# A low-rank update of 64 token tiles: 32x32 transposes of float16 pairs on VectorE and one block-diagonal projection for 16 tiles, in place of TensorE transposes

## The chip, the cores and the metric

The kernel runs on one core of one Trainium2 chip. The metric is the time of one execution on the device in microseconds; a profile's span runs from the first to the last instruction of the profiled execution.

## The reference

```python
batch, seq, d_model, r = 16, 512, 768, 16
def reference(x, A, B, scale):            # x (16, 512, 768), A (768, 16), B (16, 768), all float32; scale 0.5
    lora = np.matmul(np.matmul(x, A), B)
    return (x + scale * lora).astype(np.float32)
```

There are 8192 tokens, that is 64 tiles of 128 tokens with 768 numbers each. Read and written once, x and the output are 25.2 MB each.

## The kernel before

The 64 tiles are loaded in six parts of 2, 6, 8, 16, 16 and 16 tiles (`PARTS`). In a part of S tiles a partition holds S consecutive tokens, so that its row of a DMA is one piece of S x 3 KB. All six parts have room of their own in SBUF, and all loads and stores are issued from SyncE (SP), whose queue is worked off in program order: loads of parts 0 and 1, A and B, parts 2 to 4, then the last part, whose room first serves to prepare A and B (L87 to L93) and which is therefore loaded after that. A part is added to in place and stored from the same tile; the two last parts are stored in halves of 8 tiles (`STORES`).

The work goes by chunks of four tiles (`CHUNK`). For a chunk and each of the six blocks of 128 columns, TensorE transposes the four 128x128 float32 pieces into PSUM against an identity (`transposed`, L113), and ScalarE copies them to SBUF as float16 (L115). `projected` (L122) sums six matmuls with A as the weights into a 16x512 tile, and VectorE scales it to float16 (L127). `added` multiplies this with B (L139, a 512 and a 256 column matmul for each tile) and VectorE adds the 128x768 result to x in place (L145). The main loop puts the transposes of chunk c around the additions of chunk c-1, so that TensorE has work while ScalarE and VectorE empty PSUM. GpSimd only clears the room for A and makes the identity. `finished` issues the store of a part, or half, behind its last addition (L155).

Of the kernel before, what the change touches and what calls it, by code (L numbers as in the profile page):

```python
# [1 line left out]

# [6 lines left out]


MM_DT = mybir.dt.float16

PARTS = [2, 6, 8, 16, 16, 16]

STORES = {4: [8, 8], 5: [8, 8]}

CHUNK = 4


@with_exitstack  # L20
def kernel(
    ctx: ExitStack,
    tc: tile.TileContext,
    x: bass.AP,
    A: bass.AP,
    B: bass.AP,
    scale: bass.AP,
    out: bass.AP,
):

    nc = tc.nc
    fp32 = mybir.dt.float32
    P = 128

    x2 = x.flatten_outer_dims()
    out2 = out.flatten_outer_dims()
    T, D = x2.shape
    R = A.shape[1]  # L40
    ND = D // P
    assert D % P == 0 and sum(PARTS) * P == T
    n_splits = [(n0, min(512, D - n0)) for n0 in range(0, D, 512)]
    sc = float(scale)

    const = ctx.enter_context(tc.tile_pool(name="const", bufs=1))
    xpool = ctx.enter_context(tc.tile_pool(name="xp", bufs=1))
    xtpool = ctx.enter_context(tc.tile_pool(name="xtp", bufs=6))
    ypool = ctx.enter_context(tc.tile_pool(name="yp", bufs=2))
    ps_xt = ctx.enter_context(tc.tile_pool(name="ps_xt", bufs=3, space=bass.MemoryType.PSUM))  # L50
    ps_y = ctx.enter_context(tc.tile_pool(name="ps_y", bufs=1, space=bass.MemoryType.PSUM))
    ps_l = ctx.enter_context(tc.tile_pool(name="ps_l", bufs=2, space=bass.MemoryType.PSUM))


    parts = []
    tok = 0
    for i, S in enumerate(PARTS):
        parts.append([None, tok, S])
        tok += S * P

    def rows(t2, i):
        _, tok0, S = parts[i]
        return t2[ds(tok0, S * P), :].rearrange("(p s) d -> p s d", s=S)

    def loaded(i):
        S = parts[i][2]
        parts[i][0] = xpool.tile([P, S, D], fp32, name=f"x_sb{i}")
        nc.sync.dma_start(out=parts[i][0], in_=rows(x2, i))  # L68


    last = len(parts) - 1
    lastpool = ctx.enter_context(tc.tile_pool(name="lastp", bufs=1))
    room = lastpool.tile([P, parts[last][2], D], fp32, name="room", tag="last")
    NB = D // 32
    a_rows = room[0:32, 0, 0 : 32 * R].rearrange("b (a r) -> b a r", r=R)
    a_t = room[0:32, 1, 0 : 32 * R].rearrange("a (r b) -> a r b", r=R)
    b_f32 = room[0:R, 2, :]
    nc.gpsimd.memset(a_rows, 0.0)  # L78
    loaded(0)
    loaded(1)  # L80
    nc.sync.dma_start(out=a_rows[0:NB, :, :], in_=A.rearrange("(b a) r -> b a r", a=32))
    nc.sync.dma_start(out=b_f32, in_=B)
    for i in range(2, last):
        loaded(i)


    nc.vector.transpose(out=a_t, in_=a_rows.rearrange("b a r -> b r a"))  # L87
    a_mm = const.tile([P, ND, R], MM_DT, name="a_mm")
    a_tv = a_t[:, :, 0:NB].rearrange("a r (c k) -> a k c r", k=4)
    for k in range(4):  # L90
        nc.vector.tensor_copy(out=a_mm[ds(32 * k, 32), :, :], in_=a_tv[:, k, :, :])  # L91
    b_mm = const.tile([R, D], MM_DT, name="b_mm")
    nc.vector.tensor_copy(out=b_mm, in_=b_f32)  # L93

    parts[last][0] = lastpool.tile([P, parts[last][2], D], fp32, name="x_last", tag="last")
    nc.sync.dma_start(out=parts[last][0], in_=rows(x2, last))

    ident = const.tile([P, P], fp32, name="ident")
    make_identity(nc, ident)


    chunks = [
        (i, s0, min(CHUNK, S - s0))
        for i, (_, _, S) in enumerate(parts)
        for s0 in range(0, S, CHUNK)
    ]
    state = {}

    def transposed(c, j):
        i, s0, n = chunks[c]  # L110
        xt_ps = ps_xt.tile([P, CHUNK, P], fp32, name="xt_ps")
        for s in range(n):
            nc.tensor.transpose(xt_ps[:, s, :], parts[i][0][:, s0 + s, ds(j * P, P)], ident)  # L113
        xt_sb = xtpool.tile([P, CHUNK * P], MM_DT, name="xt_sb")
        nc.scalar.copy(out=xt_sb[:, 0 : n * P], in_=xt_ps[:, 0:n, :])  # L115
        state[c, j] = xt_sb

    def projected(c):
        n = chunks[c][2] * P
        ps_yt = ps_y.tile([R, CHUNK * P], fp32, name="ps_yt")  # L120
        for j in range(ND):
            nc.tensor.matmul(  # L122
                ps_yt[:, 0:n], a_mm[:, j, :], state.pop((c, j))[:, 0:n],
                start=(j == 0), stop=(j == ND - 1),
            )
        yt_sb = ypool.tile([R, CHUNK * P], MM_DT, name="yt_sb")
        nc.vector.tensor_scalar(  # L127
            out=yt_sb[:, 0:n], in0=ps_yt[:, 0:n], scalar1=sc, scalar2=None,
            op0=mybir.AluOpType.mult,
        )  # L130
        state[c] = yt_sb

    def added(c, subs):
        i, s0, n = chunks[c]
        subs = [s for s in subs if s < n]
        lora = {s: ps_l.tile([P, D], fp32, name="lora_ps") for s in subs}
        for s in subs:
            for n0, w in n_splits:
                nc.tensor.matmul(  # L139
                    lora[s][:, ds(n0, w)], state[c][:, ds(s * P, P)], b_mm[:, ds(n0, w)],  # L140
                    start=True, stop=True,
                )
        for s in subs:
            xs = parts[i][0][:, s0 + s, :]
            nc.vector.tensor_tensor(out=xs, in0=xs, in1=lora[s], op=mybir.AluOpType.add)  # L145

    def finished(c):
        i, s0, n = chunks[c]
        del state[c]
        end = 0  # L150
        for w in STORES.get(i, [parts[i][2]]):
            end += w
            if end == s0 + n:
                piece = slice(end - w, end)
                nc.sync.dma_start(out=rows(out2, i)[:, piece, :], in_=parts[i][0][:, piece, :])  # L155

    for c in range(len(chunks)):
        for j in range(3):
            transposed(c, j)
        if c >= 1:  # L160
            added(c - 1, (0, 1))
        for j in range(3, ND):
            transposed(c, j)
        if c >= 1:
            added(c - 1, (2, 3))
            finished(c - 1)
        projected(c)
    c = len(chunks) - 1
    added(c, (0, 1))
    added(c, (2, 3))  # L170
    finished(c)


# [1 line left out]
_INS = ['x', 'A', 'B', 'scale']  # L175
_OUTS = [((16, 512, 768), 'float32')]

_NUMBERS = {'scale': 0.5}


# [26 lines left out]
```

## Time and profile before

| | |
|---|---|
| time, median of 3 runs | 125.39 us (125.31 to 129.49) |
| span of the profiled execution | 123.3 us (its own time stands nowhere else; it is one such execution) |
| TensorE busy, matmul | 99.2 us (80%), 614 instructions |
| TensorE weight loads | 62.0 us (50%) |
| VectorE busy | 70.4 us (57%), 87 instructions |
| ScalarE busy | 52.7 us (43%), 103 instructions |
| GpSimd busy | 1.2 us (1%) |
| DMA | 50.54 MB, mean 410 GB/s over the span; the SP queue's packets took 96.5% of 16 engines' span |
| mean granted TensorE clock | 0.920 |

Busy shares are averages over the whole span. In a group's line the two numbers after the count are the busy time in us and the mean of one instruction in ns; behind the second bar stands the idle time of the engine just before these instructions, and what ended it.

### The profile page before, as it was taken

The page shows a single profiled execution, that of the slowest core. Times are in us where ns is not written, and L with a number is a line of the kernel's source. Part 1 is how long each engine was busy: PE and PEld are TensorE (multiplying, and loading weights), DVE is VectorE, ACT ScalarE, POOL GpSimd, SP SyncE. Part 2 cuts the span into 40 slices and gives each one's busy share as a digit, 9 for nine tenths or more (in the row PEclk, how much of TensorE's full clock was granted, in tenths as well). Part 3 has the DMA queues.
Part 4 walks back from the last instruction along what each step waited for, and adds up shares of the span by engine and source line. Part 5 has one row for each costly group of instructions (what it writes and reads, how often), then busy time and mean ns, then how long its engine had stood idle before and what let it go on. Part 6 is the DMA issues. An engine that isn't in the chain of part 4 may idle for free.

```text
span 123.3 us, 1614 instructions
## 1 busy us (share of the span) xinstructions
PE 99.2 (80%) x614; PEld 62.0 (50%) x614; DVE 70.4 (57%) x87; ACT 52.7 (43%) x103; POOL 1.2 (1%) x7
## 2 busy tenths in 40 slices
PE   0363999999949999999999999999999999851000
PEld 0343655566518674747475656665665747320000
DVE  0004465954886048686867577686868686884000
ACT  4060464375505555546373737364555555400000
POOL 3000000000000000000000000000000000000000
PEclk9998599999997699999999999999999999995555
DMA  4999999899989969989899999989989999998991
GB/s 155 446 407 411 399 510 478 351 436 510 415 351 510 478 290 510 452 367 446 255 421 452 432 425 526 415 383 510 388 367 438 430 423 430 425 460 359 470 399 64
DMA packets 2092, 50.54 MB, mean 410 GB/s; under 512 B 252, under 2 KB 252, under 8 KB 548
## 3 DMA queue, kind: packets, MB, share of 16 engines
q1 hardware_dynamic: 2084, 50.43, 96.5%
q8 instruction: 5, 0.08, 0.3%
q14 instruction: 3, 0.02, 0.0%
HBM read 25.26 MB, written 25.17 MB: 409 GB/s over the span
## 4 chain that ended last, share of the span: by engine, by line
PE 73%; DMA 8%; DVE 8%; issue 1%; ACT 0%; SPq 0%; ACTq 0%
PE xt_ps L113 39%; PE lora_ps L139 18%; PE ps_yt L122 17%; DMA x_sb<-in_x_dram 8%; DVE x_last L145 4%; DVE x_sb L145 3%; DVE yt_sb L127 1%; ACT xt_sb L115 0%; SPq L68 0%; ACTq L115 0%
## 5 line engine op out<-in xcount | busy, mean ns | idle before, releaser
L115 ACT CAST xt_sb<-xt_ps 128x512 f16<-128x512 f32 (+1 forms) x102 | 51.5, 567 | 52.6 <-PE xt_ps L113 46.5
L145 DVE TENSOR_TENSOR x_sb<-x_sb,lora_ps 128x768 f32<-128x768 f32 x48 | 43.5, 951 | 17.3 <-PE lora_ps L139 17.3
L113 PE MATMUL xt_ps<-ident,x_sb 128*128 128x128 f32 x288 | 40.9, 296 | 8.5 <-DMA x_sb<-in_x_dram 8.4
L113 PEld LDWEIGHTS xt_ps<-ident,x_sb 128*128 128x128 f32 x288 | 34.3, 150 | 17.5 <-issue 12.6
L139 PE MATMUL lora_ps<-b_mm,yt_sb 16*128 16x512 f16 (+1 forms) x128 | 27.0, 326 | 3.8 <-DVE yt_sb L127 1.6
L122 PE MATMUL ps_yt<-xt_sb,a_mm 128*16 128x512 f16 (+1 forms) x102 | 24.4, 376 | 0.0
L145 DVE TENSOR_TENSOR x_last<-x_last,lora_ps 128x768 f32<-128x768 f32 x16 | 14.5, 951 | 5.4 <-PE lora_ps L139 5.3
L139 PEld LDWEIGHTS <-yt_sb 16*128 16x128 f16 x128 | 9.5, 92 | 15.0 <-issue 7.5
L127 DVE TENSOR_SCALAR yt_sb<-ps_yt 16x512 f16<-16x512 f32 (+1 forms) x17 | 10.9, 642 | 8.5 <-PE ps_yt L122 8.5
L122 PEld LDWEIGHTS <-a_mm 128*16 128x16 f16 x102 | 7.9, 91 | 13.3 <-issue 5.2
L113 PE MATMUL xt_ps<-ident,x_last 128*128 128x128 f32 x96 | 12.2, 277 | 0.0
L113 PEld LDWEIGHTS xt_ps<-ident,x_last 128*128 128x128 f32 x96 | 10.3, 140 | 3.0 <-PE ps_yt L122 1.7
L87 DVE STREAM_TRANSPOSE room<-room 32x512 f32<-32x512 f32 x1 | 1.0, 1037 | 10.8 <-DMA room<-in_A_dram 10.8
L115 ACT ACT_TABLE_LOAD x1 | 1.3, 1283 | 0.7 <-PEq L188 0.7
L91 DVE CAST a_mm<-room 32x96 f16<-32x96 f32 x4 | 0.9, 233 | 0.1
L93 DVE CAST b_mm<-room 16x768 f16<-16x768 f32 x1 | 0.5, 549 | 0.0
L78 POOL MEMSET room<- 32x512 f32 x1 | 0.5, 515 | 0.3 <-POOLq L188 0.3
masks.py:199 POOL TENSOR_SCALAR_AFFINE_SELECT ident<-ident 128x128 f32<-128x128 f32 x1 | 0.3, 294 | 0.1
masks.py:197 POOL MEMSET ident<- 128x128 f32 x1 | 0.2, 194 | 0.0
L188 POOL MEMSET const-bfloat16-1.0<- 128x1 bf16 x1 | 0.1, 102 | 0.0
L188 POOL MEMSET const-uint8-127<- 128x1 uint8 x1 | 0.1, 102 | 0.0
L188 POOL MEMSET const-float32-0.0<- 128x1 f32 x1 | 0.1, 99 | 0.2 <-issue 0.2
(1 smaller groups left out, 0.1 us busy)
## 6 DMA issues: line engine op xcount, KB each, us to landing
x_sb<-in_x_dram SPq DMA_DIRECT2D x2, 6144.0 KB, 38.0
out_dram<-x_sb SPq DMA_DIRECT2D x3, 3072.0 KB, 19.9
x_last<-in_x_dram SPq DMA_DIRECT2D x1, 6144.0 KB, 50.9
out_dram<-x_sb SPq DMA_DIRECT2D x1, 6144.0 KB, 26.5
out_dram<-x_last SPq DMA_DIRECT2D x2, 3072.0 KB, 11.7
x_sb<-in_x_dram SPq DMA_DIRECT2D x1, 3072.0 KB, 15.9
x_sb<-in_x_dram SPq DMA_DIRECT2D x1, 2304.0 KB, 9.9
out_dram<-x_sb SPq DMA_DIRECT2D x1, 2304.0 KB, 44.7
```

Of the source, the lines that this page charges most:

```text
L78: nc.gpsimd.memset(a_rows, 0.0)
L87: nc.vector.transpose(out=a_t, in_=a_rows.rearrange("b a r -> b r a"))
L91: nc.vector.tensor_copy(out=a_mm[ds(32 * k, 32), :, :], in_=a_tv[:, k, :, :])
L93: nc.vector.tensor_copy(out=b_mm, in_=b_f32)
L113: nc.tensor.transpose(xt_ps[:, s, :], parts[i][0][:, s0 + s, ds(j * P, P)], ident)
L115: nc.scalar.copy(out=xt_sb[:, 0 : n * P], in_=xt_ps[:, 0:n, :])
L122: nc.tensor.matmul(ps_yt[:, 0:n], a_mm[:, j, :], state.pop((c, j))[:, 0:n], start=(j == 0), stop=(j == ND - 1),)
L127: nc.vector.tensor_scalar(out=yt_sb[:, 0:n], in0=ps_yt[:, 0:n], scalar1=sc, scalar2=None, op0=mybir.AluOpType.mult,)
L139: nc.tensor.matmul(lora[s][:, ds(n0, w)], state[c][:, ds(s * P, P)], b_mm[:, ds(n0, w)], start=True, stop=True,)
L145: nc.vector.tensor_tensor(out=xs, in0=xs, in1=lora[s], op=mybir.AluOpType.add)
L188: nc = _bacc.Bacc("TRN2", target_bir_lowering=False, num_devices=1)
```

## The change

TensorE no longer transposes. x is first narrowed to float16 in SBUF (`narrowed`, four tiles at once, 128x3072; even blocks on ScalarE, odd ones on GpSimd, L114). Two float16 neighbours are then read as one 32-bit word, and VectorE transposes the 32x32 blocks of these words in place (`turned`, 128x1536 words, L118). After that, partition 32b+i holds, for every block c of 64 columns, columns 64c+2i and 64c+2i+1 of the 32 tokens of band b. A block-diagonal matrix with A four times on its diagonal (`w_bd`, 24 matrices of 128x128, one for each c and each half k of the pair) projects all four bands at once: 24 matmuls (`projected`, L129) sum one PSUM tile of 128 x 32n for a whole group of n tiles, their moving operand being every second float16. `spread` (L140, four ScalarE instructions on 32 partitions each) scales it to float16 into the diagonal blocks of `y_bd`, and `raised` (L150) multiplies 128x128 pieces of that with B, which stands four times in `b_mm`. One VectorE addition (L157) takes two tiles, 128x1536.

The groups have 4, 12, 16, 16 and 16 tiles. There is one `xh` for all groups, two `y_bd`, two PSUM tiles for the projections and two of three banks for `raised`.

The parts are now 8, 8, 16, 16, 8 and 8 tiles, the first loaded in two halves. Parts 4 and 5 use the room of parts 0 and 1: they are loaded, from SP, after the stores of these have landed (L162 and L73), and each part is stored whole. A and B are loaded from ScalarE's queue; GpSimd clears `w_bd`, `b_mm` and both `y_bd`.

The built program holds VectorE's work in this order, T being a `turned` of four tiles and A an addition of two (the bars part the groups whose additions they are; the first T belongs to group 0, and the T's between additions of one group are turns of the next): T AA | TTT AAAAATTTTA | AATTATATAAAA | AAAATTAAATTA | AAAAAAAA. It differs for groups 1 and 3 from the order in which the source lists them. On TensorE all raised pairs of groups 1 and 3 stand ahead of the next projection; in group 2 the projection is cut in three pieces of 8 matmuls around the last two pairs.

```diff
...
 import concourse.tile as tile
 from concourse import bass_utils, mybir
 from concourse.bass import ds, ts
-from concourse.masks import make_identity
 from concourse._compat import with_exitstack
 MM_DT = mybir.dt.float16
-PARTS = [2, 6, 8, 16, 16, 16]
-STORES = {4: [8, 8], 5: [8, 8]}
-CHUNK = 4
+PARTS = [8, 8, 16, 16, 8, 8]
+ROOM = ["a", "b", "c", "d", "a", "b"]
+LOADS = {0: [4, 4]}
+GROUPS = [4, 12, 16, 16, 16]
+SUB = 4
 @with_exitstack
...
     scale: bass.AP,
     out: bass.AP,
 ):
     nc = tc.nc
     fp32 = mybir.dt.float32
     P = 128
+    Q = 32
     x2 = x.flatten_outer_dims()
     out2 = out.flatten_outer_dims()
     T, D = x2.shape
     R = A.shape[1]
-    ND = D // P
-    assert D % P == 0 and sum(PARTS) * P == T
-    n_splits = [(n0, min(512, D - n0)) for n0 in range(0, D, 512)]
+    NC = D // 64
+    GMAX = max(GROUPS)
+    assert sum(PARTS) * P == T and sum(GROUPS) == sum(PARTS)
     sc = float(scale)
     const = ctx.enter_context(tc.tile_pool(name="const", bufs=1))
     xpool = ctx.enter_context(tc.tile_pool(name="xp", bufs=1))
-    xtpool = ctx.enter_context(tc.tile_pool(name="xtp", bufs=6))
-    ypool = ctx.enter_context(tc.tile_pool(name="yp", bufs=2))
-    ps_xt = ctx.enter_context(tc.tile_pool(name="ps_xt", bufs=3, space=bass.MemoryType.PSUM))
-    ps_y = ctx.enter_context(tc.tile_pool(name="ps_y", bufs=1, space=bass.MemoryType.PSUM))
+    ypool = ctx.enter_context(tc.tile_pool(name="yp", bufs=1))
+    ps_y = ctx.enter_context(tc.tile_pool(name="ps_y", bufs=2, space=bass.MemoryType.PSUM))
     ps_l = ctx.enter_context(tc.tile_pool(name="ps_l", bufs=2, space=bass.MemoryType.PSUM))
     parts = []
+    where = []
     tok = 0
     for i, S in enumerate(PARTS):
         parts.append([None, tok, S])
+        where += [(i, s) for s in range(S)]
         tok += S * P
     def rows(t2, i):
...
     def loaded(i):
         S = parts[i][2]
-        parts[i][0] = xpool.tile([P, S, D], fp32, name=f"x_sb{i}")
-        nc.sync.dma_start(out=parts[i][0], in_=rows(x2, i))
...
+        t = xpool.tile([P, S, D], fp32, name=f"x_sb{i}", tag=ROOM[i])
+        parts[i][0] = t
+        end = 0
+        for w in LOADS.get(i, [S]):
+            nc.sync.dma_start(out=t[:, ds(end, w), :], in_=rows(x2, i)[:, ds(end, w), :])
+            end += w
+    a_rows = const.tile([Q, 64 * R], fp32, name="a_rows")
+    a_t = const.tile([Q, 2, R, Q], fp32, name="a_t")
+    b_f32 = const.tile([R, D], fp32, name="b_f32")
+    w_bd = const.tile([P, NC, 2, P], MM_DT, name="w_bd")
+    b_mm = const.tile([P, D], MM_DT, name="b_mm")
+    xh = const.tile([P, GMAX, D], MM_DT, name="xh")
+    y_bd = [const.tile([P, GMAX, P], MM_DT, name=f"y_bd{i}") for i in range(2)]
+    nc.vector.memset(a_rows, 0.0)
     loaded(0)
-    loaded(1)
-    nc.sync.dma_start(out=a_rows[0:NB, :, :], in_=A.rearrange("(b a) r -> b a r", a=32))
-    nc.sync.dma_start(out=b_f32, in_=B)
-    for i in range(2, last):
+    nc.scalar.dma_start(out=b_f32, in_=B)
+    nc.scalar.dma_start(out=a_rows[0:NC, :], in_=A.rearrange("(c e) r -> c (e r)", e=64))
+    for i in range(1, 4):
         loaded(i)
-    nc.vector.transpose(out=a_t, in_=a_rows.rearrange("b a r -> b r a"))
-    a_mm = const.tile([P, ND, R], MM_DT, name="a_mm")
...
+    nc.gpsimd.memset(w_bd.rearrange("p c k m -> p (c k m)").bitcast(fp32), 0.0)
+    nc.gpsimd.memset(b_mm.bitcast(fp32), 0.0)
+    for t in y_bd:
+        nc.gpsimd.memset(t.rearrange("p s m -> p (s m)").bitcast(fp32), 0.0)
+    nc.vector.transpose(
+        out=a_t.rearrange("i k r c -> i (k r) c"),
+        in_=a_rows.rearrange("c (i k r) -> c (k r) i", k=2, r=R),
+    )
+    for b in range(P // Q):
+        nc.vector.tensor_copy(
+            out=w_bd[ds(b * Q, Q), :, :, ds(b * Q, R)],
+            in_=a_t[:, :, :, 0:NC].rearrange("i k r c -> i c k r"),
+        )
+    for b in range(P // Q):
+        nc.vector.tensor_copy(out=b_mm[ds(b * Q, R), :], in_=b_f32)
+    starts = [sum(GROUPS[:g]) for g in range(len(GROUPS))]
+    def narrowed(g, q):
+        i, s = where[starts[g] + q * SUB]
+        engine = nc.gpsimd.tensor_copy if q % 2 else nc.scalar.copy
+        engine(out=xh[:, ds(q * SUB, SUB), :], in_=parts[i][0][:, ds(s, SUB), :])
+    def turned(q):
+        v = xh[:, ds(q * SUB, SUB), :].bitcast(fp32)
+        nc.vector.transpose(out=v, in_=v)
     state = {}
-    def transposed(c, j):
-        i, s0, n = chunks[c]
...
+    def projected(g, steps):
+        n = GROUPS[g]
+        if g not in state:
+            state[g] = ps_y.tile([P, GMAX * Q], fp32, name="ps_yt")
+        xv = xh.rearrange("p s (c j k) -> p s c j k", c=NC, k=2)
+        for m in steps:
+            c, k = divmod(m, 2)
             nc.tensor.matmul(
-                ps_yt[:, 0:n], a_mm[:, j, :], state.pop((c, j))[:, 0:n],
-                start=(j == 0), stop=(j == ND - 1),
+                state[g][:, 0 : n * Q].rearrange("p (s j) -> p s j", j=Q),
+                w_bd[:, c, k, :], xv[:, 0:n, c, :, k],
+                start=(m == 0), stop=(m == 2 * NC - 1),
             )
-        yt_sb = ypool.tile([R, CHUNK * P], MM_DT, name="yt_sb")
-        nc.vector.tensor_scalar(
...
+    def spread(g):
+        n = GROUPS[g]
+        y = state.pop(g).rearrange("p (s j) -> p s j", j=Q)
+        for b in range(P // Q):
+            q = ds(b * Q, Q)
+            nc.scalar.mul(out=y_bd[g % 2][q, 0:n, q], in_=y[q, 0:n, :], mul=sc)
+    lora = {}
+    def raised(g, p):
+        t = ps_l.tile([P, 2, D], fp32, name="lora_ps")
+        lora[g, p] = t
+        for h in range(2):
+            lhsT = y_bd[g % 2][:, 2 * p + h, :]
+            for n0, w in ((0, 512), (512, 256)) if h == 0 else ((0, 256), (256, 512)):
                 nc.tensor.matmul(
-                    lora[s][:, ds(n0, w)], state[c][:, ds(s * P, P)], b_mm[:, ds(n0, w)],
-                    start=True, stop=True,
+                    t[:, h, ds(n0, w)], lhsT, b_mm[:, ds(n0, w)], start=True, stop=True
                 )
-        for s in subs:
-            xs = parts[i][0][:, s0 + s, :]
...
+    def added(g, p):
+        i, s = where[starts[g] + 2 * p]
+        xs = parts[i][0][:, ds(s, 2), :]
+        nc.vector.tensor_tensor(out=xs, in0=xs, in1=lora.pop((g, p)), op=mybir.AluOpType.add)
+    def finished(g, p):
+        i, s = where[starts[g] + 2 * p]
+        if s + 2 == PARTS[i]:
+            nc.sync.dma_start(out=rows(out2, i), in_=parts[i][0])
+            if i == 1:
+                loaded(4)
+                loaded(5)
+    MMS = 2 * NC
+    last = len(GROUPS) - 1
+    for q in range(GROUPS[0] // SUB):
+        narrowed(0, q)
+        turned(q)
+    projected(0, range(MMS))
+    spread(0)
+    raised(0, 0)
+    for g in range(len(GROUPS)):
+        pairs = GROUPS[g] // 2
+        subs = GROUPS[g + 1] // SUB if g < last else 0
+        for q in range(subs):
+            narrowed(g + 1, q)
+        order = ["a", "a"]
+        p_left, q_left = pairs - 2, subs
+        while q_left or p_left:
+            if q_left:
+                order.append("t")
+                q_left -= 1
+                if q_left == subs - 1 and q_left and p_left:
+                    order.append("t")
+                    q_left -= 1
+            if p_left:
+                order.append("a")
+                p_left -= 1
+        p = q = 0
+        done = 0
+        after = 0
+        rest = sum(1 for o in order[max(i for i, o in enumerate(order) if o == "t"):] if o == "a") if subs else 0
+        for o in order:
+            if o == "t":
+                turned(q)
+                q += 1
+                continue
+            if p + 1 < pairs:
+                raised(g, p + 1)
+            if q == subs and subs:
+                after += 1
+                to = min(MMS, -(-MMS * after // max(1, rest - 1)))
+                projected(g + 1, range(done, to))
+                done = to
+            added(g, p)
+            finished(g, p)
+            p += 1
+        if subs:
+            projected(g + 1, range(done, MMS))
+            spread(g + 1)
+            raised(g + 1, 0)
 # ---- launch: one core; inputs and outputs as the reference has them ----
```

More of the change, by code (lines that the diff above doesn't have):

```diff
@@ L66, in loaded @@
         S = parts[i][2]
-        parts[i][0] = xpool.tile([P, S, D], fp32, name=f"x_sb{i}")
-        nc.sync.dma_start(out=parts[i][0], in_=rows(x2, i))
[L71 to L77, printed above, removed]
@@ L78 @@
-    nc.gpsimd.memset(a_rows, 0.0)
+        t = xpool.tile([P, S, D], fp32, name=f"x_sb{i}", tag=ROOM[i])
[8 more added lines that the diff above has]
+    w_bd = const.tile([P, NC, 2, P], MM_DT, name="w_bd")
@@ L84 @@
+    for i in range(1, 4):
         loaded(i)
-    nc.vector.transpose(out=a_t, in_=a_rows.rearrange("b a r -> b r a"))
-    a_mm = const.tile([P, ND, R], MM_DT, name="a_mm")
[L89 to L106, printed above, removed]
-    state = {}
-    def transposed(c, j):
-        i, s0, n = chunks[c]
[L111 to L121, printed above, removed]
+    nc.gpsimd.memset(w_bd.rearrange("p c k m -> p (c k m)").bitcast(fp32), 0.0)
[6 more added lines that the diff above has]
+    )
@@ L124, in projected @@
-                start=(j == 0), stop=(j == ND - 1),
-            )
-        yt_sb = ypool.tile([R, CHUNK * P], MM_DT, name="yt_sb")
[L127 to L136, printed above, removed]
-        for s in subs:
-            for n0, w in n_splits:
+                state[g][:, 0 : n * Q].rearrange("p (s j) -> p s j", j=Q),
@@ L139, in added @@
                 nc.tensor.matmul(
-                    lora[s][:, ds(n0, w)], state[c][:, ds(s * P, P)], b_mm[:, ds(n0, w)],
-                    start=True, stop=True,
-                )
-        for s in subs:
-            xs = parts[i][0][:, s0 + s, :]
[L145 to L171, printed above, removed]
+                    t[:, h, ds(n0, w)], lhsT, b_mm[:, ds(n0, w)], start=True, stop=True
+                )
```

## The prediction

> **What bounds the kernel now.** I read the page's forty slices first, for which resource is full; then the end of the timeline, for what sets the last microseconds; then the groups by form, for prices; then the chain and the clock by microsecond, for how a burst of TensorE runs after a pause. The slices (tenths busy; the DMA row is the mean of 16 engines):
>
> ```profile
> PE   0363999999949999999999999999999999851000
> DVE  0004465954886048686867577686868686884000
> DMA  4999999899989969989899999989989999998991
> ```
>
> Two resources are full. DMA moves 50.5 MB at a mean of 410 GB/s over the span; TensorE is busy from slice 5 on. VectorE has room: 70.4 us of 123.3. The end of the timeline (start, duration):
>
> ```profile
> 108.79 3.66 DVE L145 TENSOR_TENSOR x_last<-x_last,lora_ps 128x768 f32<-128x768 f32 x4 [0.59 <-PE lora_ps L139]
> ...
> 112.48 0.33 SPq L155 DMA_DIRECT2D out_dram<-x_last  x1
> ```
>
> The last add ends at 112.45 and the span 10.85 us later, with the store of 8 tiles. The changed kernel also ends with a store of 8 tiles, so I forecast when its last add ends and put 10.9 behind it. The prices (busy us, mean ns of one):
>
> ```profile
> L115 ACT CAST xt_sb<-xt_ps 128x512 f16<-128x512 f32 x90 | 47.3, 593 | 46.5 <-PE xt_ps L113 40.7 <-PE ps_yt L122 5.7
> L145 DVE TENSOR_TENSOR x_sb<-x_sb,lora_ps 128x768 f32<-128x768 f32 x48 | 43.5, 951 | 17.3 <-PE lora_ps L139 17.3
> ...
> L127 DVE TENSOR_SCALAR yt_sb<-ps_yt 16x512 f16<-16x512 f32 x15 | 10.1, 673 | 6.8 <-PE ps_yt L122 6.8
> ...
> L115 ACT CAST xt_sb<-xt_ps 128x256 f16<-128x256 f32 x12 | 4.2, 375 | 6.1 <-PE xt_ps L113 5.8
> ...
> L87 DVE STREAM_TRANSPOSE room<-room 32x512 f32<-32x512 f32 x1 | 1.0, 1037 | 10.8 <-DMA room<-in_A_dram 10.8
> L91 DVE CAST a_mm<-room 32x96 f16<-32x96 f32 x4 | 0.9, 233 | 0.1
> L127 DVE TENSOR_SCALAR yt_sb<-ps_yt 16x256 f16<-16x256 f32 x2 | 0.8, 408 | 1.7 <-PE ps_yt L122 1.7
> L93 DVE CAST b_mm<-room 16x768 f16<-16x768 f32 x1 | 0.5, 549 | 0.0
> L78 POOL MEMSET room<- 32x512 f32 x1 | 0.5, 515 | 0.3 <-POOLq L188 0.3
> masks.py:199 POOL TENSOR_SCALAR_AFFINE_SELECT ident<-ident 128x128 f32<-128x128 f32 x1 | 0.3, 294 | 0.1
> masks.py:197 POOL MEMSET ident<- 128x128 f32 x1 | 0.2, 194 | 0.0
> ```
>
> TensorE's prices come from the chain (start, us, what), where the same work stands once after a pause and once in full flow; the second fence is the clock by microsecond (PE, PEld, DVE, ACT and POOL busy, then the granted clock):
>
> ```profile
> 11.20 2.54 PE xt_ps L113 x12
> 13.74 1.33 PE ps_yt L122 x6
> ...
> 23.19 1.46 PE xt_ps L113 x12
> ...
> 26.86 1.39 PE ps_yt L122 x6
> ...
> 29.72 0.75 PE lora_ps L139 x4
> ```
> ```profile
> 12.00:13.00 1.00, 1.00 (x7) 1.00 (x6) 0.93 (x5) 0.00 (x0) 0.00 (x0) 0.50 1.09 467
> ...
> 15.00:16.00 1.00, 1.00 (x8) 0.70 (x8) 0.41 (x1) 0.96 (x3) 0.00 (x0) 1.00 0.92 393
> ```
>
> After an idle of 3.2 us the clock fell to 0.50 and was whole again 3.8 us after work resumed. Six 256-column matmuls took 1.33 then, six of 512 columns take 1.39 later: 0.232 us per 512 columns warm, 0.443 cold.
>
> **The change, part by part.** *Removed:* 384 TensorE transposes (53 us busy), their 102 ScalarE copies, 17 VectorE scalings. TensorE's bound is gone: warm, it has four times 24 projections of 0.232 (22 us) and 32 raised pairs of 0.75 (24 us). Bytes are unchanged, so the DMA bound stays about where the span is now; not much can be won.
>
> *VectorE* becomes the serial engine, with 32 adds of 1536 elements and 16 turns of 1536. The two scalings differ by 265 ns for 256 elements, 1.035 ns each; an add of 768 is then 156 + 795, and one of 1536 is 1.75 us. A turn is bounded above by the only transpose here: (1037-156)/512 = 1.72 ns per element, 2.80 us. But that one reads 64 bytes apart. The strided CAST pays (233-156)/96 = 0.80 ns where the dense one pays (549-156)/768 = 0.51, a factor 1.6, and 1.72 is 1.66 times 1.035. So I take the dense turn at 1.035, that is 1.75 us. Below that would be the cast's 0.51 (0.94 us), which L87 speaks against: strided against strided it is twice the cast. The Trainium skill (SBUF — State Buffer, section on Door 1) says that SBUF reads at full rate while accesses share a 16-byte line and pays at each new line: by it the dense turn costs 1.75 (sum 146), by L87's own rate 2.80 (sum 163); that line is why L87 would be dear, and no run yet shows a dense turn.
>
> *ScalarE* narrows nine blocks of 3072: slope (593-375)/256 = 0.852, fixed 157, so 2.77 us each. Its four spreads per group (32x512) are 593 each, 2.37 together. *GpSimd* narrows seven blocks: between the memset's slope (515-194)/384 = 0.836 ns (2.66 us) and the select's (294-87)/128 = 1.62 (5.05 us); I take 5.05, the row that also reads. Neither binds: in a group that starts at T the first ScalarE block is ready at T+5.1 and wanted at T+6.6; the second GpSimd block at T+10.1, wanted at T+15. Cover is lost above some 7.5 us a GpSimd block; then the third and fourth turn are late by the excess.
>
> *The hand-over.* Projection g+1 needs all turns of g+1, because each matmul runs over every tile of the group; then four spreads, then one raised pair, then VectorE may add. What VectorE still has to add after its last turn is the only cover, and the built program decides it. Its VectorE order (T turn, A add) is: T AA | TTT | AAAAATTTTA | AATTATATAAAA | AAAATTAAATTA | AAAAAAAA. Behind the last T stand 0, 0, 1, 4 and 1 adds. TensorE has paused meanwhile (its raised pairs wait for adds), so I start projections cold.
>
> *The start.* A and B move to ScalarE's queue; before, A landed at 10.8 behind 3 MB. Alone it could land near the first load's 4.4 us: B at 4.5, A at 5.5 (bounds 4.5 and 10.8). Then four casts to b_mm at 0.55, the transpose of 32x1024 strided at 1.72 (1.92), four scatters of 768 at 0.80 (0.77 each): weights at 11.7 to 12, taken as 11.9 (up to 2.6 more if a scatter runs at 1.72, up to 4.3 if A is late).
>
> *The sum*, in us from the span's start.
> - Turn to 13.65; 24 cold projections of 128 columns, weight loads showing, 3.3 (bounds 2 and 4.5); four spreads of 0.27; a cold raise 1.5: first add at 19.5, AA to 23.0.
> - TTT to 28.25 (x1 lands by 18.5, as the same 6 MB do now). Projection of 384 columns, 3.8 cold, 6.05: 34.3; spreads 1.94; raise: 37.0.
> - AAAAATTTT to 52.75; x1 finished at 54.5. Projection 3.8 cold + 15.4 x 0.232 = 7.4: 60.15; spreads 62.5; raise 63.3.
> - AATTATAT to 77.3. Under the four adds TensorE does 8 projections cold (3.54), a pair, 8, a pair, 8: 86.1; x2 finished at 86.0; spreads and raise: 89.25.
> - Eleven more to 108.5, x3 finished at 110.25; projection 7.4, spreads 2.37, raise 0.75: 119.0.
> - Eight adds: 133.0. With 10.9: span 143.9, and 2.1 that the median stands above this span now (125.4 against 123.3): 146.0.
>
> Of the 133.0, 84 is VectorE's adds and turns, 12 the start, 37 waits at five hand-overs (6, 9, 9, 3, 9, rounded).
>
> *DMA against this.* 18.9 MB at 410 GB/s after 18.5 for the first third: x3 in at 49.3. The store of x0 is issued at 40.5 and lands near 57, that of x1 near 64; on SP the load of x4 waits for the first and that of x5 for the second, landing near 71 and 79, wanted at 89 and later. Behind those two loads on SP stands x2's store, wanted only at 86. DMA then idles from 79 to 86, and before x3's store: the loss is idle DMA, not more bytes.
>
> **The rivals.**
> - *Projections at twice the price* (0.14): the clock never rises in thin bursts, or the moving operand, every second fp16, streams at the fp32 transposes' 0.95 ns a column (1.46/1536). Cold throughout adds 2.0, 3.2, 4.8, 3.2: 159; at 0.95 up to 163. For it: TensorE is busy a third of the time. Against: 3.8 us of work sufficed above.
> - *Turns at L87's rate* (0.14): 16 x 1.05 more, 163. For: the only transpose row. Against: its stride.
> - *Warm and early* (0.04): all projections warm take off 8.7, an early A two more: 135 to 137.
> - *The other side: the hand-over is short* (0.06). Place: L129 and L140 between last turn and first add. If all 37 us went, DMA would bind again near 123 to 126. It decides from 20.6 us off the 37, about 5 of the 9 at each long one. Against: spreads and raise alone are 3.1 by rows, 24 warm projections 5.6. No row gives it.
> - *The late loads bite* (0.02): x4 and x5 land 10 us or more after my 71 and 79, so that the last group's turns wait; 150 to 156. Against: 18 us of slack.
>
> **How the numbers follow.** The forecast, 146 (its own range 138 to 154), has 0.60. The range for 8 in 10 reaches down to the warm case, 136, and up through both dear cases, 164. Some 2% is what a measurement of this kernel can tell from no change, so faster is below 122.9 and slower above 127.9. Only the short hand-over gets under 127.9; of its 0.06 I give 0.04 to the DMA bound at 123 to 127.9 (same) and 0.02 to less (faster): slower 0.94.
>
> **What would show it.** Right: VectorE some 92 us busy, adds and turns near 1750 ns each; L157 waiting for lora_ps three times for about 9 us and once for 3; DMA slices below 5 between 79 and 86 and before 112; a last add near 133. Wrong: turns above 2.5 us; 512-column projections above 0.35 in the second half of a burst; VectorE waiting for GpSimd's narrowing; or DMA slices full to the end, with a time below 128.

## The result

The change makes the kernel slower: 143.27 us median (141.9 to 145.77, 4 runs) against 125.35 (125.28 to 129.49, 4 runs), ratio 1.133 with a 95% interval of 1.129 to 1.137. Here and below a ratio is taken over those runs of a kernel that lie within 1.5% of its fastest (141.9 and 142.38 here), so that it is not the quotient of the medians. The forecast was 146.0 in 136 to 164. The profiled execution took 142.38 with a span of 140.6; the forecast span was 143.9.

The page after, the slices that answer to those shown of before, and the queue:

```profile
span 140.6 us, 687 instructions
...
PE 61.6 (44%) x248; PEld 26.8 (19%) x248; DVE 87.5 (62%) x58; ACT 35.7 (25%) x30; POOL 22.8 (16%) x15
...
DVE  2659059800699991039999771999995008999000
...
PEclk9999999559999856985555799996555895599555
DMA  5999999999999799999998009999005999579992
...
q1 hardware_dynamic: 1872, 50.33, 84.7%
```

No engine is full any more. VectorE's row shows five gaps: slices 4, 8 to 9, 15 to 17, 24 and 31 to 32 (counted from 0). The DMA row, full before, has two holes of two slices each (a slice is 3.5 us). They are where the forecast put them, by the windows of that stretch (busy times, then the granted clock, the DMA share and GB/s):

```profile
79.00:84.00 5.00, 4.95 (x25) 2.20 (x23) 3.51 (x2) 0.02 (x1) 0.00 (x0) 0.99 0.00 0
86.00:98.00 12.00, 4.71 (x24) 2.33 (x25) 10.71 (x7) 5.78 (x3) 3.46 (x2) 0.92 1.06 459
98.00:107.00 9.00, 4.13 (x11) 1.36 (x11) 9.00 (x6) 0.00 (x0) 0.00 (x0) 0.50 0.00 1
```

The groups of the additions, the narrowing and the turns (busy us, mean ns, idle before and its releaser):

```profile
L157 DVE TENSOR_TENSOR x_sb<-x_sb,lora_ps 128x1536 f32<-128x1536 f32 x32 | 54.2, 1741 | 36.8 <-PE lora_ps L150 36.8
...
L114 POOL CAST xh<-x_sb 128x3072 f16<-128x3072 f32 x7 | 19.1, 2749 | 66.1 <-PE ps_yt L129 31.8
...
L118 DVE STREAM_TRANSPOSE xh<-xh 128x1536 f32<-128x1536 f32 x16 | 27.4, 1750 | 0.0
L114 ACT CAST xh<-x_sb 128x3072 f16<-128x3072 f32 x9 | 24.4, 2750 | 4.2 <-DMA x_sb<-in_x_dram 4.1
...
L97 DVE STREAM_TRANSPOSE a_t<-a_rows 32x1024 f32<-32x1024 f32 x1 | 1.9, 1932 | 1.6 <-DMA a_rows<-in_A_dram 1.6
```

Behind the start, VectorE waits 36.8 us, all in front of additions and all for a raised pair; a turn never waits. One hand-over in the chain that ended last (start, us, what):

```profile
44.82 6.76 DVE xh L118 x4
51.58 0.05 issue
51.62 7.13 PE ps_yt L129 x24
...
59.37 0.59 ACT y_bd L140
59.96 0.01 issue
59.98 0.59 ACT y_bd L140
60.56 0.01 issue
60.58 0.60 ACT y_bd L140
61.17 0.05 issue
61.22 0.84 PE lora_ps L150 x4
62.06 0.02 issue
62.08 3.42 DVE x_sb L157 x2
```

From the last turn's end to the next addition pass 10.5 us: 24 projections 7.1, four spreads 2.4, one raised pair 0.84. VectorE has a single addition (1.7) to put there. The timeline of VectorE at its end:

```profile
105.62 1.71 DVE L157 TENSOR_TENSOR x_sb<-x_sb,lora_ps 128x1536 f32<-128x1536 f32 x1
116.44 13.40 DVE L157 TENSOR_TENSOR x_sb<-x_sb,lora_ps 128x1536 f32<-128x1536 f32 x8 [9.11 <-PE lora_ps L150]
```

The last add ends at 129.84 (forecast 133.0), and the span ends 10.8 us later, as before.

### The profile page after: what moved, and what is told of

Same layout as the page of the kernel before. It is cut to its first block, busy times and chain, and to the rows that moved or that the text cites. A ratio compares the mean times of both kernels' runs of the same rounds, so it can differ in the third digit from the quotient of the medians.

```text
span 140.6 us, 687 instructions
## 1 busy us (share of the span) xinstructions
PE 61.6 (44%) x248; PEld 26.8 (19%) x248; DVE 87.5 (62%) x58; ACT 35.7 (25%) x30; POOL 22.8 (16%) x15
## 4 chain that ended last, share of the span: by engine, by line
DVE 51%; PE 25%; ACT 6%; DMA 5%; issue 4%; DVEq 1%; ACTq 0%
DVE x_sb L157 29%; PE ps_yt L129 21%; DVE xh L118 19%; ACT y_bd L140 6%; DMA a_rows<-in_A_dram 5%; PE lora_ps L150 4%; DVE a_t L97 1%; DVE w_bd L102 1%; DVEq L246 1%; DVE a_rows L86 1%; ACTq L246 0%; ACTq L140 0%; DVEq L97 0%; ACTq L114 0%
## 5 line engine op out<-in xcount | busy, mean ns | idle before, releaser
L157 DVE TENSOR_TENSOR x_sb<-x_sb,lora_ps 128x1536 f32<-128x1536 f32 x32 | 54.2, 1741 | 36.8 <-PE lora_ps L150 36.8
L150 PE MATMUL lora_ps<-b_mm,y_bd 128*128 128x512 f16 (+1 forms) x128 | 31.8, 387 | 32.3 <-DVE x_sb L157 21.4
L129 PE MATMUL ps_yt<-xh,w_bd 128*128 128x512 f16 (+2 forms) x120 | 30.4, 424 | 33.5 <-DVE xh L118 33.5
L114 POOL CAST xh<-x_sb 128x3072 f16<-128x3072 f32 x7 | 19.1, 2749 | 66.1 <-PE ps_yt L129 31.8
L140 ACT ACTIVATE y_bd<-ps_yt 32x512 f16<-32x512 f32 (+2 forms) x20 | 10.1, 503 | 73.1 <-PE ps_yt L129 72.9
L118 DVE STREAM_TRANSPOSE xh<-xh 128x1536 f32<-128x1536 f32 x16 | 27.4, 1750 | 0.0
L114 ACT CAST xh<-x_sb 128x3072 f16<-128x3072 f32 x9 | 24.4, 2750 | 4.2 <-DMA x_sb<-in_x_dram 4.1
L150 PEld LDWEIGHTS <-y_bd 128*128 128x128 f16 x128 | 13.6, 110 | 50.4 <-issue 33.9
L129 PEld LDWEIGHTS <-w_bd 128*128 128x128 f16 x120 | 13.2, 119 | 49.8 <-issue 22.7
L107 DVE CAST b_mm<-b_f 16x768 f16<-16x768 f32 x4 | 2.2, 550 | 2.8 <-DMA b_f<-in_B_dram 2.7
L97 DVE STREAM_TRANSPOSE a_t<-a_rows 32x1024 f32<-32x1024 f32 x1 | 1.9, 1932 | 1.6 <-DMA a_rows<-in_A_dram 1.6
```

Source lines behind the costliest of these rows:

```text
L97: nc.vector.transpose(out=a_t.rearrange("i k r c -> i (k r) c"), in_=a_rows.rearrange("c (i k r) -> c (k r) i", k=2, r=R),)
L107: nc.vector.tensor_copy(out=b_mm[ds(b * Q, R), :], in_=b_f32)
L114: engine(out=xh[:, ds(q * SUB, SUB), :], in_=parts[i][0][:, ds(s, SUB), :])
L118: nc.vector.transpose(out=v, in_=v)
L129: nc.tensor.matmul(state[g][:, 0 : n * Q].rearrange("p (s j) -> p s j", j=Q), w_bd[:, c, k, :], xv[:, 0:n, c, :, k], start=(m == 0), stop= ...
L140: nc.scalar.mul(out=y_bd[g % 2][q, 0:n, q], in_=y[q, 0:n, :], mul=sc)
```

## The experiments

Three theories were set against each other. *Chain:* VectorE's serial order and its waits at the hand-overs set the end. *Room:* the last 16 tiles wait for stores, and the idle DMA that this makes sets the end. *Clock:* TensorE, idle between bursts, runs its projections at half clock, and that is the price. The four runs of the change spread over 4 us, and kernels with its order do much the same (e12: 140.86 to 144.86), so the range stands beside each median. In e1, e2, e5, e6 and e12 the order of VectorE's and TensorE's work is held as the changed kernel has it, so that the edit cannot move it.

**Short turns (e1)**

```diff
-        v = xh[:, ds(q * SUB, SUB), :].bitcast(fp32)
+        v = xh[:, ds(q * SUB, SUB), 0:64].bitcast(fp32)
```

> Each turn transposes only the first 64 of 768 columns (128 words in place of 1536), everything else and its order on every engine is as in the changed kernel; the other columns enter the projection unturned. Chain theory (VectorE's serial order and the hand-overs set the end): a turn falls from about 1.69 to about 0.3 us, 16 of them take off about 22 us, until the DMA stream binds near a span of 120 to 122; time 121 to 125, against 142.4 of the changed kernel. Room theory (the last 16 tiles' wait for stores and the idle DMA it makes set the end): little moves, above 138. Clock theory (TensorE's cold projections are the price): unchanged within 2, 141 to 145.

125.1 us (124.78 to 125.64), ratio to the kernel before 0.998 (0.995 to 1.001). The turns, the last additions and the queue of this kernel:

```profile
L120 DVE STREAM_TRANSPOSE xh<-xh 128x128 f32<-128x128 f32 x16 | 4.1, 291 | 0.2 <-ACT xh L116 0.2
...
91.61 13.41 DVE L160 TENSOR_TENSOR x_sb<-x_sb,lora_ps 128x1536 f32<-128x1536 f32 x8 [7.17 <-PE lora_ps L152]
...
q1 hardware_dynamic: 1872, 50.33, 95.4%
```

A turn took 0.29 us and the last add ended at 105.0 in place of 129.8: 25 us came off the chain, and only 17 to 18 off the time, because DMA binds then (407 GB/s over a span of 123.9). VectorE still waited 34.8 us for raised pairs. So its serial work and these waits together were the bound, and the DMA stream stands just where the kernel before ends. Room and clock fall as the main cause: the loads still waited for the stores, and the projections of the two hand-overs with the longest waits still took 6.4 and 6.9 us.

**No reload (e2)**

```diff
-                loaded(4)
-                loaded(5)
+                parts[4][0] = parts[0][0]
+                parts[5][0] = parts[1][0]
```

> The last 16 tiles are not loaded; the kernel works a second time on the tiles of parts 0 and 1, so 6.3 MB and the wait of the last loads for the first stores are gone; order on all engines as in the changed kernel. Chain theory: nothing moves, 141 to 144.5. Room theory: some 8 to 15 us come off, 127 to 135. Clock theory: nothing moves.

145.18 us median (142.3 to 145.8), as the change's own runs (141.9 to 145.77). Taking away 6.3 MB and both waits brings nothing: the room theory is out for this kernel.

**Reuse alone, in the kernel before (e7)**

```diff
-PARTS = [2, 6, 8, 16, 16, 16]
+PARTS = [2, 6, 8, 16, 16, 8, 8]
...
+                if i == 2:
+                    loaded(5)
+                    loaded(6)
```

Part 5 takes the room of parts 0 and 1, part 6 that of part 2.

> The kernel before with one part of the change alone: the last 16 tiles load over the room of the first 16, behind their stores; TensorE transposes as before. Chain theory: the reuse costs nothing that is seen, 124.5 to 127. Room theory: the loads' wait for the stores leaves DMA idle, 130 or more.

126.54 us (126.27 to 126.58), ratio 1.011 (1.008 to 1.014). So this half of the change, on the old engines, costs 1.4 us at most. DMA does not work longer: its queue is busy for 119.0 us in both kernels (96.5% of 123.3, 95.4% of 124.7), so what is added is idle DMA, and its slices show it ahead of the last store. The last add ended at 114.3 in place of 112.45, behind a stretch near 87 us where the built order has 24 TensorE transposes in one go and VectorE waits 2.8 us; how much of the 1.4 belongs to the reuse itself was not separated.

**The order of the source (e3)**: every VectorE and TensorE instruction of groups' work is pinned behind the one before it in the source.

```diff
-        nc.vector.transpose(out=v, in_=v)
+        tc.keep_in_program_order(nc.vector.transpose(out=v, in_=v))
```
(and so for L129, L150 and L157)

> VectorE and TensorE hold their work in the order in which the source lists it: AATTATATAA for group 1 and AATTATATAAAA for group 3, so 2 adds in place of 1 stand behind the last turn of group 2's tiles and 4 in place of 1 behind the last turn of group 4's. Chain theory: the wait before group 2 falls from 8.9 to about 7.2, that before group 4 from 9.1 to about 5 in all; about 6 us off, 135.5 to 138. Room theory: no gain, 141 to 145. Clock theory: the same bursts are as cold, 141 to 145.

139.83 us (139.61 to 140.1), ratio 1.118 (1.112 to 1.123): a gain, but under half of the 6 us expected. The chain did as told. The waits fell from 8.9 to 7.0 and from 9.1 to 3.3 plus 0.6, and the last add ended at 123.05, 6.8 us earlier. But the span ended 14.8 us behind it, not 10.8. The timeline of this kernel shows why:

```profile
98.81 5.16 DVE L158 TENSOR_TENSOR x_sb<-x_sb,lora_ps 128x1536 f32<-128x1536 f32 x3
104.60 1.75 DVE L158 TENSOR_TENSOR x_sb<-x_sb,lora_ps 128x1536 f32<-128x1536 f32 x1 [0.64 <-PE lora_ps L150]
109.64 13.41 DVE L158 TENSOR_TENSOR x_sb<-x_sb,lora_ps 128x1536 f32<-128x1536 f32 x8 [3.29 <-PE lora_ps L150]
```

The additions that cover the hand-over are the last ones of part 3, whose 6.3 MB store leaves only behind them, at 106.35 (107.3 in the change). DMA had nothing to do until then and has 12.6 MB to write afterwards: 137.8 - 106.35 = 31.4 us. I drew from this a second bound: the span is the later of last add + 10.8 and part 3's end + 31.4. For the change itself the two are 140.6 and 138.7, so the first held by only 2 us. The next runs test it.

**The order of the source, 16-tile parts stored in halves (e9)**

```diff
-        if s + 2 == PARTS[i]:
-            nc.sync.dma_start(out=rows(out2, i), in_=parts[i][0])
+        if (s + 2) % 8 == 0:
+            piece = slice(s - 6, s + 2)
+            nc.sync.dma_start(out=rows(out2, i)[:, piece, :], in_=parts[i][0][:, piece, :])
```

> The order of the source (as in e3) and the two parts of 16 tiles stored in halves of 8 as soon as these are added. Two-bound theory (the span is the later of last add + 10.8 and of the issue of part 3's store + the DMA time of the 12.6 MB then left, 31.4): e3 was held by the second, its last add at 123.05 would allow 133.9; with halves the second bound falls by about 7 and the time goes from 139.8 to 135 to 137. If something else ate e3's gain: unchanged, 139 to 141.

135.92 us (134.51 to 137.0), ratio 1.079 (1.073 to 1.084). The last add ended at 122.4 and the span 10.3 later. The rest of e3's gain is there.

**Halves in the built order (e12)**: the same edit on the change, with its own order.

> The changed kernel with nothing but the parts of 16 tiles stored in halves. Two-bound theory: its last add binds by about 2 us (129.85 + 10.8 against 107.35 + 31.4), so it does not gain: 141.5 to 145.5, as the changed kernel's own runs. If the late stores set its end: 135 to 139.

143.18 us (140.86 to 144.86), ratio 1.127 (1.121 to 1.134): no gain to be seen, as the chain's bound says.

**Projection by quarters (e4)**

```diff
-    def projected(g, steps):
+    def projected(g, q):
+        t = ps_y.tile([P, GMAX * Q], fp32, name="ps_yt")
...
+                y, w_bd[:, c, k, :], xv[:, ds(q * SUB, SUB), c, :, k],
...
+                nc.scalar.mul(out=y_bd[g % 2][r, ds(q * SUB, SUB), r], in_=y[r, :, :], mul=sc)
```

Behind each turn stand 24 matmuls of 128 columns and four spreads, in place of 24 matmuls of up to 512 columns behind the last one; the order on the other engines is held too.

> The projection of a group is done by quarters: 24 matmuls of 128 columns and four spreads of 32x128 as soon as one block of four tiles is turned, in place of 24 matmuls of 512 columns and four spreads of 32x512 behind the last turn. Orders of VectorE's adds and turns as in the changed kernel. Chain theory: a hand-over falls from about 10.5 us (7.2 + 2.4 + 0.85) to about 4.7 or less, and is hidden where four adds follow; 17 to 21 us off in all until the DMA stream binds, 121 to 127. Room theory: above 138. Clock theory: four thinner bursts stay colder than one long one, no gain, 140 or more.

125.87 us median of 10 (125.31 to 129.02), ratio 1.003 (1.000 to 1.007). The edit moves not one VectorE instruction and takes 17 us off. The waits of VectorE, first of the change, then of this kernel (us in total, times, longest):

```profile
DVE x_sb L157 <- PE lora_ps L150: 36.8, 7, 9.1
```
```profile
DVE x_sb L156 <- PE lora_ps L148: 14.3, 7, 5.0
```

Its last additions, that of part 3 first:

```profile
90.11 1.72 DVE L156 TENSOR_TENSOR x_sb<-x_sb,lora_ps 128x1536 f32<-128x1536 f32 x1
93.75 13.41 DVE L156 TENSOR_TENSOR x_sb<-x_sb,lora_ps 128x1536 f32<-128x1536 f32 x8 [1.93 <-PE lora_ps L148]
```

The last add came 22.7 us earlier, at 107.2, and was no longer what bound: part 3's end at 91.8 + 31.4 is 123.2, the span 123.7.

**Quarters and cover together (e8)**: the orders AATTATATAA, AATTATATAAAA and AAAATTAATTAA.

> Projection by quarters, and an order with adds behind the last turn: AATTATATAA, AATTATATAAAA, AAAATTAATTAA. Chain theory: hand-overs 2 to 4 are hidden, the last add ends near 105, before DMA has moved its 50 MB: DMA binds, span 117 to 122, time 119 to 124, at or below the kernel before (125.4). Room theory: above 130.

130.08 us (129.53 to 131.48), ratio 1.038 (1.034 to 1.042): worse than e4, and a miss. Its windows (as above) show the hole:

```profile
80.00:88.00 8.00, 5.50 (x56) 4.72 (x55) 6.36 (x5) 3.29 (x9) 1.21 (x1) 0.79 0.97 418
89.00:96.00 7.00, 5.84 (x56) 4.89 (x57) 4.92 (x4) 2.15 (x8) 0.00 (x0) 0.76 0.16 67
```

Two additions behind the last turn covered the hand-over and finished part 3 only at 96.3, since its last raised pair stood behind the last quarter's projection on TensorE. 96.3 + 31.4 is 127.7; the span was 127.8. What I had expected to be cover delayed the store.

**e4 and e8 with halves (e10, e11)**

> Projection by quarters (as in e4) and the parts of 16 tiles stored in halves. Two-bound theory: e4 is held by the DMA stream and a hole of some 2 us ahead of part 3's store; the hole is filled, 123.5 to 125.0, against 125.5 of e4 and 125.1 of the kernel before. If DMA holds it in any case: 125.0 to 126.

> As e8, with the parts of 16 tiles stored in halves. Two-bound theory: e8's last add at 109.6 allows a span near 120.5, its part 3 was finished only at 96.3 (+31.4 = 127.7, the span was 127.8); with halves the first half goes out near 79 and DMA has no hole: 124 to 126.5. If e8 lost its time elsewhere: 129.5 to 131.

125.16 us (124.81 to 125.61), ratio 0.997 (0.994 to 1.000), and 125.26 us (124.94 to 125.56), ratio 0.998 (0.994 to 1.001). The hole is gone in e10, whose slices read:

```profile
DVE  2549605991699997799997999994993999920000
...
DMA  4999997999799798999999999999999999999980
...
q1 hardware_dynamic: 2160, 50.33, 96.0%
```

For e10 that is the time expected if DMA holds it in any case. Both arrive at the kernel before and not below it in any way that can be measured. The changed way of computing is no slower once its hand-overs are short, and no faster, because the 50.5 MB at 408 to 409 GB/s fill the span either way. So no version tried here beats the kernel before.

**TensorE kept busy (e5)**: useless matmuls into the next group's PSUM tile while VectorE turns.

```diff
+            tc.keep_in_program_order(nc.tensor.matmul(
+                state[g][:, :], w_bd[:, 0, 0, :], b_mm[:, 0:512], start=True, stop=True
+            ))
```

> TensorE does useless 512-column matmuls into the next group's PSUM tile while VectorE turns: 24 ahead of the projections of groups 1 and 2, 8 ahead of that of group 4; all else as in the changed kernel. If the pause is what makes a projection dear: 384 columns fall from 5.9 to about 4.2 us, 512 columns from 7.1 and 7.4 to about 5.4, together about 5 us off, 136 to 139.5. If the clock is no matter (room theory, or the projections are slow by their strided operand): 141 to 145.

138.88 us (137.3 to 140.56), ratio 1.101 (1.095 to 1.107). TensorE's timeline of this kernel, the three projections (start, duration, count, idle before):

```profile
28.66 4.13 PE L133 MATMUL ps_yt<-xh,w_bd 128*128 128x384 f16 x24 [0.79 <-DVE xh L122]
...
50.90 7.07 PE L133 MATMUL ps_yt<-xh,w_bd 128*128 128x512 f16 x24 [2.35 <-DVE xh L122]
...
105.72 5.41 PE L133 MATMUL ps_yt<-xh,w_bd 128*128 128x512 f16 x24 [1.67 <-DVE xh L122]
```

After a pause of 0.8 and 1.7 us the projections took 4.1 and 5.4, in place of 5.9 and 7.4; after 2.35 us nothing was won. So the clock's share is real, 1.7 to 2 us a projection, and it is a part of the hand-overs and not their cause: 3.7 us for the two that gained, and 4.4 between the medians, where the quarters brought 17. The profile is that of the longest of the four executions (140.56 us); whether the middle projection gained in the shorter ones is not shown.

**GpSimd twice (e6)**

```diff
+        if q % 2:
+            engine(out=xh[:, ds(q * SUB, SUB), :], in_=parts[i][0][:, ds(s, SUB), :])
         engine(out=xh[:, ds(q * SUB, SUB), :], in_=parts[i][0][:, ds(s, SUB), :])
```

> GpSimd does each of its seven narrowings twice (5.5 us a block in place of 2.75), order on all engines as in the changed kernel. Chain theory: the second result of a group is ready about 11 us behind the projection's end and wanted 15 or more behind it; nothing moves, 141 to 145. If GpSimd's narrowing set the start of the turns: 5 us or more for each of three groups, 155 or more.

144.65 us (143.34 to 145.5), ratio 1.153 (1.146 to 1.159), a little above the change's 1.133. In the trace, of the run with 145.5, no turn waits for GpSimd, whose two blocks of a group now take 11 us. VectorE waits 39.6 us for raised pairs; in e2's trace, at 145.3 us and with GpSimd as in the change, it is 39.7. So the cover claimed for GpSimd was there, and the longer time shows up in waits that e2 has too; why they are 2.8 us above the change's 36.8 was not tested.

## Why the prediction was right

The side, the size and the mechanism held: VectorE became a serial engine, and each group is handed over through TensorE and ScalarE before it may add.

- *Adds and turns.* Taken at 1.75 each; they measure 1741 and 1750 ns. The dense turn runs at the add's rate, and the strided one, L97 now, at 1932 for 1024 elements, (1932-156)/1024 = 1.73 ns, the 1.72 of L87 again, where the dense turn has (1750-156)/1536 = 1.04. So the rival of 163 us falls. That the stride made L87 dear fits, but both strided rows also have 32 partitions where the turn has 128, and no run parts the two. The Trainium skill (SBUF — State Buffer, section on Door 1) has full rate within a 16-byte line and a price for each new line; the trace agrees (1.04 against 1.72 and 1.73).
- *The mis-sized term of the sum* is here too. Instructions that follow each other overlap: eight adds take 13.40, 1.675 each, so 48 of them cost 80.4 and not 84. That is the bulk of the 3.2 us by which the last add was early, and VectorE is busy 87.5 us for the 92 named as a sign. The rows of before had shown it, four adds in 3.66 where four times 951 is 3.80.
- *Hand-overs.* Forecast 37 in all, measured 36.8; singly 5.0, 8.9, 8.9, 1.7 and 3.3, 9.1 (the 1.7 stand between additions of group 2, and the forecast's list of five leaves them out while its sum has them). The projections were 5.87, 7.13 and 7.36 for 6.05, 7.4 and 7.4, so the rival with projections at twice the price falls too. The half-clock start was right, as e5 shows from the other side. The Trainium skill (TensorE: Matmul & The Clock Gate, section on HAM oscillation) has the same pattern, bursts between waits that each start cold; the trace agrees (granted clock 0.50 from 52 to 55 us, after a pause of 7.5 us).
- *The start* came out by luck, by errors that nearly cancel. A landed at 8.4 and not at 5.5, and the scatters have 384 elements and not the 768 that I counted (0.47 us each, not 0.77): weights at 12.4 for 11.9. The first hand-over then took 5.0 for 5.85, and the first add began at 19.2 for 19.5.
- *GpSimd* was taken at the select's rate, 5.05; it ran at the memset's, 2.75. Nothing depended on it (e6).
- *The end.* 10.8 behind the last add for 10.9. The DMA holes were foreseen at 79 and ahead of part 3's store, but only as idle time. That part 3's late store is a second bound, 1.9 us below the first, was not seen; it did not touch the forecast and spoiled my expectations for e3 and e8.
- *The rivals.* The short hand-over was ruled out by its price, and rightly for this kernel; e4 shows that its place was right, since with it DMA binds at 125.9, inside the 123 to 126 given for it. The late loads cost nothing (e2).

## What to carry to other kernels

When an engine works through groups in order, count for each group what stands between its last input and the next output, and what other work the built order leaves there: here shortening such gaps was worth 17 us. Cutting the step into quarters took the waits from 36.8 to 14.3 us, where a faster step (e5) brought some 4 us. Work that covers a gap is also someone's last work: look what store or transfer waits behind it before moving it. And where a resource was full over the whole span, as DMA was here, relieving another one can at best bring the time back to it.

## What was not expected of the hardware

- At the start of a run the clock row and the matmuls do not fit together: in the window from 14 to 17 us the row reads 1.00, while 24 matmuls of 128 columns took 2.72 us; the same 24 take 1.54 later in e8. Whether the row is wrong there or something else slows this burst, no run shows.
- The length of the pause alone does not decide how a projection of 512 columns starts. A pause of 2.35 us behind 5.3 us of full work cost as much as one of 7.5 us (7.07 against 7.13, e5 and the change). A pause of 1.67 us behind 2.1 us of useless matmuls cost nothing (5.41, e5), and one of 1.66 us behind raised pairs with pauses of 0.9 us between them cost it again (6.93, e1).
- The moving operand that takes every second float16 streams at the rate of a packed one: 5.41 us for 24 x 512 columns are 0.225 us per 512, as the projection before (0.232).
